# Attention ramp of a hybrid encoder: three shifted copies issued ahead of the rotations, new due times for the rotations and for two value tiles

## The chip, the cores and the metric

The kernel is one program on one core of a Trainium2 chip. The metric is the device time of one execution in microseconds (us). Before the change its median was 1796.95 us of three runs (1796.52 to 1799.05).

## The reference, cut to what matters

A trunk of two layers over 512 tokens and 16 meta tokens (T = 528), width 2048, in float32. Layer 0, which the change touches, is softmax attention with 16 query heads, 8 key and value heads and rotary positions; layer 1 is gated linear attention.

```python
def attention_mixer(h, w_in, q_norm, k_norm, w_out, ang_row, ang_col):
    q, k, v, gate = jnp.split(h @ w_in, [...], axis=-1)
    q = apply_axial_rope(rmsnorm(q, q_norm), ang_row, ang_col)   # per head of 128
    k = apply_axial_rope(rmsnorm(k, k_norm), ang_row, ang_col)
    ...
    s = jnp.einsum('bqkgd,bskd->bkgqs', qb, k) * (ATTN_HEAD_DIM ** -0.5)
    p = jax.nn.softmax(s.astype(jnp.float32), axis=-1).astype(v.dtype)
    o = jnp.einsum('bkgqs,bskd->bqkgd', p, v)
    ...
    return (o * jax.nn.silu(gate)) @ w_out

def rmsnorm(x, w):
    y = xf * lax.rsqrt(jnp.mean(xf * xf, axis=-1, keepdims=True) + NORM_EPS)
    return y * w

def _rotate(x, ang):            # on each half of a head, split in two again
    return jnp.concatenate([x1 * cos - x2 * sin, x2 * cos + x1 * sin], axis=-1)
```

## The kernel before, in words

Every float32 product is made of three fp32r products: each operand is split into a high part (a cast on ACT, L129) and a low part (a subtraction on DVE, L130), and TensorE does high x high, high x low and low x high (L152 to L154). Activations live as `uh`, `ul`, 16 tiles of 128 channels by 528 tokens. `project` (L147 is its weight load) makes one 128-channel tile of an input projection: two halves of 264 columns, for each 16 channel tiles by 3 products, 96 matmuls in all. Its weights come as two units of 512 KB (`wraw`, two buffers), each split into `whi` and `wlo` (three buffers each).

Work beside the projections (softmax, rotations, transposes) is emitted by a clock that the program keeps while it is built: `clk.step` adds the modelled duration of each three matmuls, and `clk.after(dt, fn)` emits `fn` when the modelled time has advanced by `dt`. `tc.high_priority` lets weight splits be placed earlier. After that each engine runs its own list in order; semaphores hold an instruction until its operands, or the buffer it writes, are free.

Layer 0 first makes 13 gate tiles (the last ten by seven products in place of eight, `seven`, L229 to L231), then runs attention in eight groups. A group is one key and value head and two query heads. While group g's softmax runs, the projections of group g+1 (v for g+1 = 1 first, then k, q, q) keep TensorE busy: `qkv` and `values`.

One head's **rotation** is `rope` (L290). With x the projected head and w its norm weight it takes `qw` = w x and `sq` = x squared. Four DMAs on the GpSimd (POOL) queue copy `qw` into `qs` with neighbouring blocks of 32 partitions swapped: the shifted copy (L294). POOL multiplies `qw` by cos (L299) and `qs` by sin (L300). `sq` is split into `sh`, `sl` (one buffer each), and two pairs of matmuls with a matrix of ones, `ssq` (L304, L305), sum it over the head, a pair for each half of the tokens. DVE scales that into `f`, which is `sq` again (L307); ACT makes the inverse root (L133, L134); DVE adds (L311), multiplies (L312), and the result is split into `kh`, `kl` or `qh`, `ql`. `steps` are three due times: first pair of sums, second pair, and the rest (`late`).

The first group has no projections of its own at that point: its k and two q heads (`qws`, three tiles; numbers 94, 95, 96 in the order shown below) were made at the start of the program and wait. `first_group` (L575) squares, scales and rotates them one after the other, 4.2 clock us apart, then yields 9.0 before group 0's softmax. Beside it TensorE runs the v tile and the k tile of group 1. This stretch, from the last `seven` product to the first score matmul (L613), is called the ramp here.

`values(g)` (L540) transposes the projected v tile on TensorE into `vps` and `vpm` (L550, L557), from which ACT and DVE make `vh`, `vl` and `vm` (L553 to L561). Group 0's v tile was projected just before the ramp into the one tile `vt`; group 1's goes into the same `vt`. The transposes and the second pair of `ssq` of the ramp share two PSUM banks (`ps_t`, tag "t"); the first pair of `ssq` uses `ps_o`.

`stored_gates` (L583) loads gate tiles of earlier groups from DRAM into `gr` (two buffers) by DMAs of the SP queue, which also carries all weight loads.

Of the kernel before, what the change touches and what calls it, by code (L numbers as in the profile page):

```python
# [10 lines left out]
F32 = mybir.dt.float32  # L11
F32R = mybir.dt.float32r
I32 = mybir.dt.int32
AF = mybir.ActivationFunctionType
# [5 lines left out]
P = 128  # L20
# [62 lines left out]
def hybrid_encoder(  # L83
# [203 lines left out]
            A.activation(sq[:, a:b], ps, AF.Square)  # L287
        return qw, sq, evac

    def rope(qw, sq, outs, steps, banks):  # L290
        qs = wk.tile([P, T], F32, tag="qs", name="qs")
        for b in range(4):
            s = b ^ 1
            nc.gpsimd.dma_start(out=qs[b * 32:b * 32 + 32, :], in_=qw[s * 32:s * 32 + 32, :])  # L294
        sh = wk.tile([P, T], F32R, tag="sh", name="sh", bufs=1)
        sl = wk.tile([P, T], F32R, tag="sl", name="sl", bufs=1)
        split(sh, sl, sq)
        f = sq
        G.tensor_tensor(qw, qw, cos, op=ALU.mult)  # L299
        G.tensor_tensor(qs, qs, sin, op=ALU.mult)  # L300

        def sums(bank, a, b):
            ps = bank[0].tile([P, 512], F32, tag=bank[1], name="ssq")[:, :b - a]
            PE.matmul(ps, ones_r, sh[:, a:b], start=True, stop=False)  # L304
            PE.matmul(ps, ones_r, sl[:, a:b], start=False, stop=True)  # L305
            with tc.high_priority(AHEAD):
                V.scalar_tensor_tensor(f[:, a:b], ps, 1.0 / P, erow[:, a:b], op0=ALU.mult, op1=ALU.add)  # L307

        def late():
            rsqrt_inplace(f)  # L310
            V.tensor_tensor(qw, qw, qs, op=ALU.add)  # L311
            V.tensor_tensor(qw, qw, f, op=ALU.mult)  # L312
            for hi, lo, a, b in outs:
                split(hi, lo, qw[:, a:b])
        for step, bank, part in zip(steps, banks, HALVES):
            clk.after(step, lambda bank=bank, part=part: sums(bank, *part))
        clk.after(steps[2], late)
# [8 lines left out]
    Q1 = T + META  # L326

    qws = [c0.tile([P, T], F32, name=f"qw{i}") for i in range(3)]
    vt = c0.tile([P, T], F32, name="vt")

    st = ExitStack()
    sp = pool(st, "start")
# [167 lines left out]
    for h in range(3):  # L500
        y = yp.tile([P, T], F32, tag=f"y{h % 2}", name="y")
        project(w_in0, 4096 + h * P, HALVES, lambda ps, a, b: A.copy(y[:, a:b], ps))
        nc.gpsimd.dma_start(out=g_d[h], in_=y)
    project(w_in0, 3072, HALVES, lambda ps, a, b: A.copy(vt[:, a:b], ps))
    clk.finish(built)
    free = [wpool.tile([P, 1024], F32, tag="wraw", name="wraw", bufs=2) for _ in range(2)]
    free += [q[:, :1024] for q in quarters]
# [22 lines left out]
    NP = 3  # L530
    REP = 80
    pn_bufs = [pb.tile([P, T + 96], F32, name=f"pn{i}") for i in range(NP)]
    for t in pn_bufs:
        G.memset(t, 0.0)
    vm_bufs = [pb.tile([REP, P], F32R, name=f"vm{i}") for i in range(2)]
    for t in vm_bufs:
        G.memset(t.bitcast(F32), 0.0)
# [2 lines left out]
    def values(g):  # L540
        vh = wa.tile([P, 4, P], F32R, tag="vh", name="vh")
        vl = wa.tile([P, 4, P], F32R, tag="vl", name="vl")
        vm = vm_bufs[g % 2]
        if g:
            project(w_in0, 3072 + g * P, HALVES, lambda ps, a, b: A.copy(vt[:, a:b], ps))

        def late():
            ps = ps_t.tile([P, 512], F32, tag="t", name="vps")
            for t in range(4):
                PE.transpose(ps[:, t * P:(t + 1) * P], vt[:, t * P:(t + 1) * P], ident)  # L550
            for t in range(4):
                pst = ps[:, t * P:(t + 1) * P]
                A.activation(vh[:, t, :], pst, AF.Copy, scale=rcol[:, t:t + 1])  # L553
                V.scalar_tensor_tensor(vl[:, t, :], pst, rcol[:, t:t + 1], vh[:, t, :].bitcast(F32),
                                       op0=ALU.mult, op1=ALU.subtract)
            pm = ps_t.tile([P, 512], F32, tag="t", name="vpm")[:META, :P]
            PE.transpose(pm, vt[:, SEQ:T], ident)  # L557
            rm = rcol[:META, 4:5]
            A.activation(vm[0:META], pm, AF.Copy, scale=rm)
            A.activation(vm[64:64 + META], pm, AF.Copy, scale=rm)  # L560
            V.scalar_tensor_tensor(vm[32:32 + META], pm, rm, vm[0:META].bitcast(F32),  # L561
                                   op0=ALU.mult, op1=ALU.subtract)
        clk.after(1.2 if g else 2.0, late)
        return vh, vl, vm

    def qkv(g):
        qk, outs = qks[g % 2]
        vv = values(g) if g == 1 else None
        for i, c in enumerate((2048 + g * P, 2 * g * P, (2 * g + 1) * P)):
            qw, sq, evac = take(col(KN if i == 0 else QN))  # L570
            project(w_in0, c, HALVES, evac)
            rope(qw, sq, outs[i], (3.2, 8.8, 9.6), ((ps_p, "pp"), (ps_p, "pp")))
        return qk, vv or values(g)

    def first_group():  # L575
        for i in range(3):
            sq = wk.tile([P, T], F32, tag="sq", name="sq")
            A.activation(sq, qws[i], AF.Square)
            A.activation(qws[i], qws[i], AF.Copy, scale=col(QN if i else KN))
            rope(qws[i], sq, qks[0][1][i], (2.6, 3.9, 8.3), ((ps_o, "o"), (ps_t, "t")))  # L580
            yield 4.2 if i < 2 else 9.0

    def stored_gates(hs, held):  # L583

# [129 lines left out]
    last_gs = [gate(14)]  # L714


    slots = qws + [vt] + [wk.tile([P, T], F32, tag=tag, name="ogr") for tag in ("qs", "sq")]
    NS = len(slots)

    def load_og(k):  # L720
# [694 lines left out]
```

## Time and profile before

| what | value |
|---|---|
| median of three runs | 1796.95 us |
| the profiled execution | 1796.57 us |
| its span in the profile | 1794.8 us |
| TensorE (PE) busy | 1759.3 us |
| VectorE (DVE) busy | 1120.7 us |
| ScalarE (ACT) busy | 946.6 us |
| GpSimd (POOL) busy | 256.6 us |
| mean granted TensorE clock | 0.997 |
| attention groups in the span | from 208.55 to about 800 us |

PE is the matmul stream, PEld its weight loads. A row of the timeline gives the start, the duration, the engine, the line, what is written from what, and in brackets how long the engine had been idle and what ended that. Matmuls overlap: each lasts 0.28 us in the rows, while the next starts about 0.12 us after it, so lost time is read from start to start.

### The profile page before, as it was taken

How to read it: one execution, taken by the hardware profiler on the slowest of the kernel's cores; microseconds unless marked ns; L12 is line 12 of the kernel's file. 1: busy time of each engine (PE TensorE's matmuls, PEld its weight loads, DVE VectorE, ACT ScalarE, POOL GpSimd, SP SyncE). 2: the span in 40 equal slices, each digit the busy share in tenths (PEclk: the TensorE clock that was granted, in tenths of full speed). 3: DMA queues.
4: the chain of work that ended last, by engine and by line, in shares of the span. 5: the costliest groups of instructions: out<-in, count | busy, mean ns of one | idle time of the engine just before them, and what ended most of it. 6: DMA issues, size and time to landing. Idle time of an engine off the chain costs nothing. (4 is left out here: it accounts for less than half of the span.)

```text
span 1794.8 us, 31607 instructions
## 1 busy us (share of the span) xinstructions
PE 1759.3 (98%) x12591; PEld 1655.3 (92%) x12591; DVE 1120.7 (62%) x1904; ACT 946.6 (53%) x1909; POOL 256.6 (14%) x366
## 2 busy tenths in 40 slices
PE   8999989999999999999999999999999999999998
PEld 8999989999999999999999899988898989888886
DVE  5877687667666666732237887667684865764224
ACT  5543466556556454633238544477685765863221
POOL 3000333322312211121111101110000000000000
PEclk9999999999999999999999999999999999999999
DMA  8444423223232233343336444343232333254223
GB/s 254 128 133 124 131 84 102 83 85 107 72 96 84 84 89 91 121 124 89 99 90 207 120 126 133 93 135 96 83 113 83 101 95 89 83 159 176 94 94 129
DMA packets 265252, 200.95 MB, mean 112 GB/s; under 512 B 9772, under 2 KB 239856, under 8 KB 264576
## 3 DMA queue, kind: packets, MB, share of 16 engines
q1 hardware_dynamic: 251888, 159.54, 30.9%
q0 software_dynamic: 13216, 39.39, 6.4%
q8 instruction: 99, 1.62, 0.4%
q14 instruction: 49, 0.40, 0.1%
HBM read 164.39 MB, written 28.01 MB: 107 GB/s over the span
## 5 line engine op out<-in xcount | busy, mean ns | idle before, releaser
L152 PE MATMUL pp<-uh,whi 128*128 128x264 f32 (+1 forms) x2320 | 713.1, 308 | 0.2
L153 PE MATMUL pp<-ul,whi 128*128 128x264 f32 (+1 forms) x2320 | 703.7, 303 | 1.5 <-DVE ul L423 1.5
L154 PE MATMUL pp<-uh,wlo 128*128 128x264 f32 (+1 forms) x2320 | 703.7, 303 | 0.4 <-POOL wlo L362 0.3
L130 DVE TENSOR_TENSOR wlo<-wraw,whi 128x1024 fp32r<-128x1024 f32 (+1 forms) x239 | 292.8, 1226 | 289.6 <-ACT whi L129 286.7
L154 PEld LDWEIGHTS pp<-uh,wlo 128*128 128x128 f32 x2320 | 438.2, 189 | 17.5 <-POOL wlo L362 0.6
L152 PEld LDWEIGHTS pp<-uh,whi 128*128 128x128 f32 x2320 | 438.2, 189 | 16.8 <-ACT uh L422 0.5
L153 PEld LDWEIGHTS pp<-ul,whi 128*128 128x128 f32 x2320 | 438.5, 189 | 15.5 <-DVE ul L423 2.0
L129 ACT CAST whi<-wraw 128x1024 fp32r<-128x1024 f32 (+1 forms) x239 | 248.9, 1042 | 279.2 <-PE pp L153 92.2
L621 ACT ACTIVATE pn<-s,mx 128x528 f32<-128x528 f32 (+1 forms) x72 | 50.2, 697 | 87.5 <-DVE mx L618 87.4
L129 ACT CAST whi<-x 128x1024 fp32r<-128x1024 f32 x48 | 50.1, 1046 | 70.6 <-PE pp L230 52.0
L294 POOL DMA_DIRECT2D qs<-qw x96 | 48.5, 510 | 246.9 <-ACT sq L287 212.3
L1327 PE MATMUL f<-whi,ul 128*128 128x512 f32 x192 | 75.6, 394 | 0.0
L1325 PE MATMUL f<-whi,uh 128*128 128x512 f32 x192 | 75.5, 393 | 0.0
L1326 PE MATMUL f<-wlo,uh 128*128 128x512 f32 x192 | 75.3, 392 | 0.0
L231 PE MATMUL pp<-uh,wlo 128*128 128x264 f32 x264 | 75.2, 285 | 0.0
L229 PE MATMUL pp<-uh,whi 128*128 128x264 f32 x264 | 75.0, 284 | 0.0
L230 PE MATMUL pp<-ul,whi 128*128 128x264 f32 x264 | 74.7, 283 | 0.0
L130 DVE TENSOR_TENSOR wlo<-x,whi 128x1024 fp32r<-128x1024 f32 x48 | 58.6, 1222 | 22.1 <-ACT whi L129 22.1
L311 DVE TENSOR_TENSOR qw<-qw,qs 128x528 f32<-128x528 f32 x24 | 20.0, 835 | 69.1 <-POOL qs L300 69.1
L636 DVE TENSOR_TENSOR pl<-pT,ph 128x512 fp32r<-128x512 f32 (+1 forms) x80 | 47.4, 592 | 16.5 <-ACT ph L635 15.6
L229 PE MATMUL pp<-th,whi 128*128 128x264 f32 x192 | 56.1, 292 | 0.8 <-ACT th L129 0.8
L618 DVE TENSOR_REDUCE mx<-s 128x1 f32<-128x528 f32 (+1 forms) x72 | 50.6, 702 | 9.5 <-PE s L615 8.4
(403 smaller groups left out, 3746.7 us busy)
## 6 DMA issues: line engine op xcount, KB each, us to landing
wraw<-in_attn_w_in_dram SPq DMA_DIRECT2D x82, 512.0 KB, 4.2
wraw<-in_gla_w_in_dram SPq DMA_DIRECT2D x81, 512.0 KB, 3.9
wraw<-in_attn_w_out_dram SPq DMA_DIRECT2D x32, 512.0 KB, 3.8
wraw<-in_gla_w_out_dram SPq DMA_DIRECT2D x32, 512.0 KB, 3.8
x<-in_gla_w_in_dram SPq DMA_DIRECT2D x15, 512.0 KB, 4.3
qs<-qw POOLq DMA_DIRECT2D x96, 66.0 KB, 4.0
x<-in_attn_w_in_dram SPq DMA_DIRECT2D x12, 512.0 KB, 4.6
x<-h_d SPq DMA_DIRECT2D x32, 132.0 KB, 2.9
```

What stands on the lines that cost most here:

```text
L129: A.copy(hi, src)
L130: V.tensor_tensor(lo, src, hi.bitcast(F32), op=ALU.subtract)
L152: PE.matmul(ps, wh, uh[:, k, a:b], start=first, stop=False)
L153: PE.matmul(ps, wh, ul[:, k, a:b], start=False, stop=False)
L154: PE.matmul(ps, wl, uh[:, k, a:b], start=False, stop=last)
L229: PE.matmul(ps, w[0][:, k], bh[:, k], start=k == 0, stop=False)
L230: PE.matmul(ps, w[0][:, k], bl[:, k], start=False, stop=False)
L231: PE.matmul(ps, w[1][:, k], bh[:, k], start=False, stop=k == KH - 1)
L618: V.reduce_max(mx, s, axis=AX.XY, negate=True)
L1325: PE.matmul(ps, uh[:, k, ts], wh[:, kk], start=(k == 0), stop=False)
L1326: PE.matmul(ps, uh[:, k, ts], wl[:, kk], start=False, stop=False)
L1327: PE.matmul(ps, ul[:, k, ts], wh[:, kk], start=False, stop=(k == KT - 1))
```

## The change

Four edits. (1) The four DMAs of a shifted copy move from `rope` into `shifted`, whose tile `qs` gets three buffers in place of two; `first_group` now squares, scales and copies all three heads, then clears the three `pn` tiles, and only then rotates. The third head's squares take one of the two `gr` buffers. (2) The due times of the rotations of the ramp go from (2.6, 3.9, 8.3), 4.2 apart, to (2.6, 4.4, 9.6), 4.6 apart, and softmax starts 9.8 after the last in place of 9.0. (3) Group 0's v tile is transposed at 10.5 clock us in place of 2.0, and group 1's v tile gets the other `gr` buffer (`vt1`) in place of the shared tile. (4) In all later groups the first pair of `ssq` is due 4.0 after its head's projection in place of 3.2. At the end of attention the six tiles that take reloaded data are the same kinds, with "sq" and "qs" in the other order.

```diff
-    def rope(qw, sq, outs, steps, banks):
-        qs = wk.tile([P, T], F32, tag="qs", name="qs")
+    def shifted(qw):
+        qs = wk.tile([P, T], F32, tag="qs", name="qs", bufs=3)
         for b in range(4):
             s = b ^ 1
             nc.gpsimd.dma_start(out=qs[b * 32:b * 32 + 32, :], in_=qw[s * 32:s * 32 + 32, :])
+        return qs
+
+    def rope(qw, sq, outs, steps, banks, qs=None):
+        qs = qs or shifted(qw)
...
-    for t in pn_bufs:
-        G.memset(t, 0.0)
...
+        vt = wa.tile([P, T], F32, tag="gr", name="vt1") if g == 1 else vt0
...
-        clk.after(1.2 if g else 2.0, late)
+        clk.after(1.2 if g else 10.5, late)
...
-            rope(qw, sq, outs[i], (3.2, 8.8, 9.6), ((ps_p, "pp"), (ps_p, "pp")))
+            rope(qw, sq, outs[i], (4.0, 8.8, 9.6), ((ps_p, "pp"), (ps_p, "pp")))
...
     def first_group():
+        sqs, qss = [], []
         for i in range(3):
-            sq = wk.tile([P, T], F32, tag="sq", name="sq")
-            A.activation(sq, qws[i], AF.Square)
+            sqs.append(wk.tile([P, T], F32, tag="sq", name="sq") if i < 2 else
+                       wa.tile([P, T], F32, tag="gr", name="sq"))
+            A.activation(sqs[i], qws[i], AF.Square)
             A.activation(qws[i], qws[i], AF.Copy, scale=col(QN if i else KN))
-            rope(qws[i], sq, qks[0][1][i], (2.6, 3.9, 8.3), ((ps_o, "o"), (ps_t, "t")))
-            yield 4.2 if i < 2 else 9.0
+            qss.append(shifted(qws[i]))
+        for t in pn_bufs:
+            G.memset(t, 0.0)
+        for i in range(3):
+            rope(qws[i], sqs[i], qks[0][1][i], (2.6, 4.4, 9.6), ((ps_o, "o"), (ps_t, "t")), qss[i])
+            yield 4.6 if i < 2 else 9.8
...
-    slots = qws + [vt] + [wk.tile([P, T], F32, tag=tag, name="ogr") for tag in ("qs", "sq")]
+    slots = qws + [vt0] + [wk.tile([P, T], F32, tag=tag, name="ogr") for tag in ("sq",)]
+    slots.append(wk.tile([P, T], F32, tag="qs", name="ogr", bufs=3))
```

What this does to the engines' lists is not what the code's order alone says, so three places are shown. Lines of the changed kernel are 4 higher at L299 and L300 (L303, L304), L304 and L305 (L308, L309), L307, L311 and L312 (L311, L315, L316).

POOL at the ramp, before; `qw_94` is the key head, `qw_95` and `qw_96` the query heads, and `g_d<-y` stores a gate tile:

```order
L294 DMA qs<-qw_94 32x528 x4
L294 DMA qs<-qw_95 32x528
L512 DMA g_d<-y_2148 128x528
L294 DMA qs<-qw_95 32x528
L299 TENSOR_TENSOR qw_94<-qw_94,cos 128x528
L300 TENSOR_TENSOR qs<-qs,sin 128x528
L294 DMA qs<-qw_95 32x528 x2
L299 TENSOR_TENSOR qw_95<-qw_95,cos 128x528
L300 TENSOR_TENSOR qs<-qs,sin 128x528
L601 TENSOR_TENSOR gs<-gs,gr 128x528
L294 DMA qs<-qw_96 32x528 x4
L299 TENSOR_TENSOR qw_96<-qw_96,cos 128x528
```

The same place of POOL after the change:

```order
L294 DMA qs<-qw_94 32x528 x4
L294 DMA qs<-qw_95 32x528
L516 DMA g_d<-y_2148 128x528
L294 DMA qs<-qw_95 32x528 x3
L303 TENSOR_TENSOR qw_94<-qw_94,cos 128x528
L304 TENSOR_TENSOR qs<-qs,sin 128x528
L294 DMA qs<-qw_96 32x528 x4
L303 TENSOR_TENSOR qw_95<-qw_95,cos 128x528
L304 TENSOR_TENSOR qs<-qs,sin 128x528
L303 TENSOR_TENSOR qw_96<-qw_96,cos 128x528
L304 TENSOR_TENSOR qs<-qs,sin 128x528
L610 TENSOR_TENSOR gs<-gs,gr 128x528
```

Two copies of the second head and all four of the third have moved ahead of the second head's multiplications; the third head's copies still stand behind the first head's multiplications. The five clearing instructions ahead of these rows are the same five in both.

DVE at the ramp, before, from the first `vm` on (its rows ahead of that split the k tile's first weights, in both kernels):

```order
L561 SCALAR_TENSOR_TENSOR vm_2412<-vpm,rcol,vm_2412 16x128
L311 TENSOR_TENSOR qw_94<-qw_94,qs 128x528
L307 SCALAR_TENSOR_TENSOR sq<-ssq,erow 128x264
L554 SCALAR_TENSOR_TENSOR vl<-vps,rcol,vh 128x128
L307 SCALAR_TENSOR_TENSOR sq<-ssq,erow 128x264
L554 SCALAR_TENSOR_TENSOR vl<-vps,rcol,vh 128x128
L130 TENSOR_TENSOR sl<-sq,sh 128x528
L591 TENSOR_TENSOR gr<-gr,rrow 128x528
```

The same place of DVE after the change:

```order
L311 SCALAR_TENSOR_TENSOR sq<-ssq,erow 128x264
L315 TENSOR_TENSOR qw_94<-qw_94,qs 128x528
L311 SCALAR_TENSOR_TENSOR sq<-ssq,erow 128x264
L130 TENSOR_TENSOR sl<-sq,sh 128x528
L316 TENSOR_TENSOR qw_94<-qw_94,sq 128x528
L311 SCALAR_TENSOR_TENSOR sq<-ssq,erow 128x264
L130 TENSOR_TENSOR kl_2380<-qw_94,kh_2379 128x528
L315 TENSOR_TENSOR qw_95<-qw_95,qs 128x528
L130 TENSOR_TENSOR wlo<-wraw,whi 128x1024
L311 SCALAR_TENSOR_TENSOR sq<-ssq,erow 128x264
L130 TENSOR_TENSOR sl<-sq,sh 128x528
L315 TENSOR_TENSOR qw_96<-qw_96,qs 128x528
```

The work on the v tiles (L554, L561) and on the gates (L591) has left this stretch; what remains are the rotations and the k tile's second weights.

PE in a later group (the first half's sums of a query head, then the transposes `pT`, `pTm` of softmax rows), before:

```order
L304 MATMUL ssq<-sh,ones_r 128x264
L305 MATMUL ssq<-sl,ones_r 128x264
L152 MATMUL pp<-uh,whi 128x264
L153 MATMUL pp<-ul,whi 128x264
L154 MATMUL pp<-uh,wlo 128x264
L631 MATMUL pT<-ident,pn_2408 128x128 x4
L633 MATMUL pTm<-ident,pn_2408 80x128
```

After the change, from the same matmul on:

```order
L152 MATMUL pp<-uh,whi 128x264
L153 MATMUL pp<-ul,whi 128x264
L154 MATMUL pp<-uh,wlo 128x264
L640 MATMUL pT<-ident,pn_2408 128x128 x4
L642 MATMUL pTm<-ident,pn_2408 80x128
L152 MATMUL pp<-uh,whi 128x264
L153 MATMUL pp<-ul,whi 128x264
L154 MATMUL pp<-uh,wlo 128x264
L308 MATMUL ssq<-sh,ones_r 128x264
L309 MATMUL ssq<-sl,ones_r 128x264
```

The pair of sums now stands six matmuls and five transposes later. From group 2 on the other pairs of sums either stay or stand six matmuls later, and nothing else on PE has moved; beyond attention every engine's list is the same.

More of the change, by code (lines that the diff above doesn't have):

```diff
@@ L328, in hybrid_encoder @@
     qws = [c0.tile([P, T], F32, name=f"qw{i}") for i in range(3)]
-    vt = c0.tile([P, T], F32, name="vt")
+    vt0 = c0.tile([P, T], F32, name="vt0")
     st = ExitStack()
@@ L503, in hybrid_encoder @@
         nc.gpsimd.dma_start(out=g_d[h], in_=y)
-    project(w_in0, 3072, HALVES, lambda ps, a, b: A.copy(vt[:, a:b], ps))
+    project(w_in0, 3072, HALVES, lambda ps, a, b: A.copy(vt0[:, a:b], ps))
     clk.finish(built)
```

## The prediction

> **What bounds the kernel now.** I read the busy times first, then the chain of work that ended last, then TensorE by stretches of time.
>
> ```profile
> PE 1759.3 (98%) x12591; PEld 1655.3 (92%) x12591; DVE 1120.7 (62%) x1904; ACT 946.6 (53%) x1909; POOL 256.6 (14%) x366
> PE 12%; ACT 1%; DVE 0%; DMA 0%; issue 0%; DVEq 0%
> 100.00:200.00 100.00, 100.00 (x825) 100.00 (x824) 72.76 (x83) 36.88 (x41) 4.34 (x8) 1.00 0.38 114
> 208.55:240.60 32.05, 25.37 (x181) 24.52 (x179) 22.37 (x34) 18.27 (x38) 16.67 (x17) 0.89 0.48 139
> 212.84:216.25 3.41, 1.31 (x11) 1.10 (x10) 2.38 (x2) 1.61 (x4) 3.09 (x2) 1.00 0.06 21
> 216.25:219.66 3.41, 3.41 (x18) 3.41 (x18) 2.65 (x6) 1.57 (x4) 1.44 (x3) 0.52 0.83 257
> 226.49:229.90 3.41, 0.36 (x1) 0.19 (x1) 3.41 (x8) 1.10 (x3) 2.01 (x4) 1.00 0.57 162
> 229.90:233.32 3.42, 2.73 (x12) 2.73 (x13) 3.36 (x5) 2.39 (x5) 1.92 (x2) 0.52 0.53 155
> 301.58:305.00 3.42, 1.70 (x14) 1.49 (x13) 3.10 (x5) 2.62 (x6) 0.00 (x0) 1.00 0.00 0
> 305.00:308.41 3.41, 3.41 (x30) 3.41 (x30) 3.28 (x9) 2.61 (x6) 1.14 (x3) 1.00 0.54 157
> ```
>
> PE is busy 98% and makes up the end of the chain too, so only what lets PE wait, or clocks it down, can shorten the kernel. Undisturbed, 825 matmuls fill 100 us: 0.1212 us from start to start. The ramp is the exception. In 32.05 us PE issues 178 instructions by my count of its list (156 projection matmuls, 12 sums, 10 transposes; the row says 181), worth 21.6 us: some 10.5 us are lost. The last six rows show a second loss, the clock: a stretch of 3.41 us with 1.31 or 0.36 us of matmuls is followed by one at 0.52 of full speed (about 1.7 us lost each), one with 1.70 is not.
>
> PE's waits from 243 to 800 us (total, times, longest), and then, from the timeline, the matmuls of the ramp that waited, with the first score matmul:
>
> ```profile
> PE s L613 <- ACT pn L621: 4.3, 6, 1.7
> PE ssq L305 <- DVE sl L130: 2.6, 5, 0.5
> PE pT L631 <- DVE pl L636: 1.4, 2, 1.2
> ...
> 215.97 0.39 PE L304 MATMUL ssq<-sh,ones_r 128*128 128x264 f32 x1 [2.10 <-DVE vm L561]
> 227.36 0.36 PE L304 MATMUL ssq<-sh,ones_r 128*128 128x264 f32 x1 [1.20 <-DVE sq L307]
> 230.59 0.59 PE L305 MATMUL ssq<-sl,ones_r 128*128 128x264 f32 x1 [2.88 <-DVE sl L130]
> 240.60 0.28 PE L613 MATMUL s<-kh,qh 128*128 128x264 f32 x1
> ```
>
> All three waits of the ramp are for DVE, which works one list through: first `vm`, then the first head's sums, then `sl` of the third head behind a weight split.
>
> **Part 1, the ramp (edits 1 to 3).** DVE and POOL take turns:
>
> ```profile
> 205.82 2.01 POOL L294 DMA_DIRECT2D qs<-qw  x4 [0.17 <-issue]
> 213.16 1.30 POOL L299 TENSOR_TENSOR qw<-qw,cos 128x528 f32<-128x528 f32 x1 [2.61 <-DMA qs<-qw]
> 213.50 2.04 DVE L130 TENSOR_TENSOR wlo<-wraw,whi 128x1024 fp32r<-128x1024 f32 x1 [4.31 <-ACT whi L129]
> 214.42 2.29 POOL L300 TENSOR_TENSOR qs<-qs,sin 128x528 f32<-128x528 f32 x1
> 216.66 1.03 POOL L294 DMA_DIRECT2D qs<-qw  x2
> 226.56 2.01 POOL L294 DMA_DIRECT2D qs<-qw  x4 [0.52 <-ACT sh L129]
> 227.75 0.69 DVE L591 TENSOR_TENSOR gr<-gr,rrow 128x528 f32<-128x528 f32 x1
> 228.71 1.21 DVE L130 TENSOR_TENSOR wlo<-wraw,whi 128x1024 fp32r<-128x1024 f32 x1
> 229.85 0.69 DVE L130 TENSOR_TENSOR sl<-sq,sh 128x528 fp32r<-128x528 f32 x1
> 231.22 0.43 DVE L307 SCALAR_TENSOR_TENSOR sq<-ssq,erow 128x264 f32<-128x264 f32 x1
> 233.72 1.83 DVE L312 TENSOR_TENSOR qw<-qw,sq 128x528 f32<-128x528 f32 x1
> ```
>
> The same `wlo` takes 1.21 us alone and 2.04 beside POOL: it starts to work when cos ends (214.46) and ends at 215.54, and POOL's sin, 2.29 instead of 1.30, starts only then. DVE at L312 stretches from 0.7 to 1.83 likewise, while L307, which reads PSUM, keeps 0.43. So of two instructions with both operands in SBUF, one waits for the whole other. The Trainium skill ("SBUF — State Buffer", section "Who interferes with whom") says just this of DVE's tensor_tensor and GpSimd, a lock for the whole instruction; it speaks against this change, which puts three heads' multiplications back to back; by it this part gains 3.1, without it 8.0 (both worked out below from rows).
>
> The changed order, walked. The first cos waits for copies issued earlier, so it stays at 213.16; two more copies (1.03) lie in POOL's 2.61 of waiting. `wlo` ends at 215.54 and sin at 216.71; then L311 and L307, and `sl` of the second head ends at 218.45. The v tile's transposes and its `vm` are gone from here, so PE does not stop at 213.9. It reaches the sum that needs `sl` after 71 instructions, at 208.55 + 71 × 0.1212 = 217.15: **first wait 1.3**. POOL then issues the third head's four copies (2.01, to 218.75), and from there cos and sin of heads two and three (four of 1.30) alternate with DVE's L312 (0.70), `kl` (0.65), L311 (0.60), the k tile's second `wlo` (1.20) and L307 (0.40): 5.2 + 3.55 from 218.75 is 227.5. PE needs that last L307's bank for `vpm`, where it stands at 222.6: **second wait 4.9**. The stretch 223.08 to 226.49 is then empty, and PE runs at half speed from 227.5 to 229.90: **1.2**. Together 7.4.
>
> The first score matmul now stands 15 projection matmuls later, after 193 instructions (23.4 us). Before, that work would take 32.05 + 15 × 0.1212 = 33.9; now 23.4 + 7.4 = 30.8. **Gain 3.1.** With each multiplication at its short length the same walk has waits of 0.4, 1.15 and 0.95 and no slow stretch: gain 8.0. At the other end the multiplications displace one more sum, for one or two more slow stretches (1.7 each): gain 1.4 to below nothing (-0.3). I take 3.1, since the stretched rows stand in this very place.
>
> Given back: the gates' multiplications (L591) leave the ramp for group 0's softmax, whose `gr` loads wait until the other uses of `gr` are done. POOL's five clearings stay ahead of the first copy: nothing. The weight loads queued behind `gr` on SP are needed some 20 us later: nothing. For DVE's later start in group 0 I charge **0.6**, one L591 (0.69), with bounds 0 and 1.7 (the longest wait of a score matmul for exp, above). Part 1 in sum: **2.5**.
>
> **Part 2, 4.0 in place of 3.2.** The later groups lose at one place each, five times:
>
> ```profile
> 414.89 0.28 PE L154 MATMUL pp<-uh,wlo 128*128 128x264 f32 x1
> 415.11 0.39 PE L304 MATMUL ssq<-sh,ones_r 128*128 128x264 f32 x1
> 416.01 0.39 PE L305 MATMUL ssq<-sl,ones_r 128*128 128x264 f32 x1 [0.51 <-DVE sl L130]
> 416.23 0.28 PE L152 MATMUL pp<-uh,whi 128*128 128x264 f32 x1
> 427.07 0.29 PE L613 MATMUL s<-kh,qh 128*128 128x264 f32 x1
> ...
> 414.92 0.29 DVE L638 TENSOR_TENSOR pmt<-pTm,pmt 16x128 fp32r<-16x128 f32 x1
> 415.24 0.71 DVE L130 TENSOR_TENSOR sl<-sq,sh 128x528 fp32r<-128x528 f32 x1
> ```
>
> From 414.89 to 416.23 are 1.34 us where three starts should take 0.36: 0.98 lost, though the wait says 0.51. The pair now stands six matmuls and five transposes later (some 1.3 us), so PE reaches it at about 416.3 to 416.5, and `sl` is done at 415.95. What is late next: `pT`, now 1.2 us earlier, whose DVE operands are done at 415.21; then nothing before the next score matmul, at 427.07. 5 × 0.98 = 4.9; I take **4.7**, for a `pT` that waits a little; bounds 1 (it waits as `ssq` did) and 5.
>
> **Part 3, the boundary of groups 0 and 1.**
>
> ```profile
> 281.01 0.29 PE L305 MATMUL ssq<-sl,ones_r 128*128 128x264 f32 x1
> 302.80 0.28 PE L154 MATMUL pp<-uh,wlo 128*128 128x264 f32 x1
> 304.80 0.39 PE L613 MATMUL s<-kh,qh 128*128 128x264 f32 x1 [1.72 <-ACT pn L621]
> ...
> 286.38 0.71 DVE L130 TENSOR_TENSOR ql<-qw,qh 128x528 fp32r<-128x528 f32 x1
> ```
>
> The second score of group 1 waits for an exponential and loses 2.00 - 0.12 = 1.88. In the changed order 98 PE instructions instead of some 41 lie between first and second score, so that goes. But the first score now stands 46 instructions (5.1 to 5.6 us) after the pair of sums whose head it reads, and from that pair to the end of `ql` it takes 287.09 - 281.01 = 6.1: a new wait of about 1.0. **Gain 0.9**, bounds -1.9 and 1.9.
>
> **Sum.** 2.5 + 4.7 + 0.9 = 8.1 off the profiled 1796.57 us (its span 1794.8, with 1.8 around it): 1788.5. That execution lies 0.4 below the median, which I leave in the range. What this kernel's measurement can tell from no change is about 0.2%, 3.6 us: faster begins below 1793.4.
>
> **Rivals.** (a) *The waits of the ramp only move.* Two more slow stretches (3.4) eat the 3.1: about 1791 to 1792. For it: 1.31 us of matmuls in a stretch were not enough to keep the clock, and the second wait is twice as long as the longest now. Against: the walk has the slow stretch in it already, and three blocked places become two. The Trainium skill ("TensorE: Matmul & The Clock Gate", section "What's actually happening") has half rate follow a whole idle window; here one with 1.31 us of matmuls was enough, so the measurement decides; by that rule (a) would need two more empty stretches, and my sum, whose stretch is empty, stays.
>
> (b) *POOL and DVE don't meet.* If the splits fall into POOL's pauses, the ramp gains up to 8.0: 1783.6. Against: every pair of rows that overlaps in the ramp is stretched.
>
> (c) *The step to 4.0 doesn't pay*, because `pT` or the next pair waits in place of `ssq`: gain 1 or less, about 1792 to 1793. For it: `pT L631` waited before, 1.2 us at most. With (a) together: some 1796, no change.
>
> (d) *Slower: the copies land late.* The first four copies were issued from 205.82 to 207.83 and the first cos started at 213.16, 5.3 us on, while weights and cos and sin tables were under way. Now up to twelve copies share that time. Each us that cos starts later passes to sin, L311, `sl` and PE's first and second wait. From 8.1 us late the gain is used up, and at 12 us it is 1796.57 - 8.1 + 12 = 1800.5. Against: the first head's copies are still ahead of all others on their queue.
>
> (e) *It doesn't do what it says*: the third head's copies stand behind the first head's multiplications on POOL, not first. That is in the walk: without it those 2.01 us before the second cos would go.
>
> **How the numbers follow.** Forecast 1788.5 with 0.52; (a) 0.17, (b) 0.07, (c) 0.12, of which half below 1793.4, (a) with (c) 0.06, (d) 0.06. Faster: 0.52 + 0.17 + 0.07 + 0.06 = 0.82; no change 0.06 + 0.06 = 0.12; slower 0.06. The range leaves out (d), (a) with (c) and the better half of (b), and takes in (c) and most of the bounds: 1784.5 to 1794.0.
>
> **What would show it.** Right: the first two sums of the ramp without a wait for `vm`; a wait of 1 to 1.5 us near 217 for `sl` and one of 4 to 5 near 223 for L307's result, with one stretch at half clock behind it; no wait of L309 for `sl` after 300 us; the wait for exp at 304.8 gone, and about 1 us at the first score of group 1. Wrong: a slow stretch more or none (part 1 by 1.7 or more), five waits of `pT` near 0.5 us (part 2), or a first cos later than 213.5 (rival d).

## The result and the profile after

| | before | changed |
|---|---|---|
| median of 15 runs each | 1798.20 us | 1801.32 us |
| lowest to highest | 1795.35 to 1799.58 | 1798.70 to 1807.04 |
| profiled execution | 1796.57 us | 1803.56 us |

The ratio is 1.0021, 95% interval 1.0013 to 1.0029: slower by some 3.8 us, where 8.1 us of gain were forecast. The profiled execution of the changed kernel is 2.2 us above its median, that of the kernel before 1.6 us below, so the two traces differ by 7.0 us where the medians differ by 3.1. Two executions of all those on record, one of the kernel before (1892 us) and one of the version called "changed, all three" below (4421 us), were far off the others and are left out of the ratios and of that version's median.

The page of the changed kernel begins as before; PE is as busy, in a longer span:

```profile
span 1801.8 us, 31618 instructions
...
PE 1759.4 (98%) x12591; PEld 1655.7 (92%) x12591; DVE 1125.4 (62%) x1904; ACT 946.1 (53%) x1909; POOL 256.3 (14%) x366
```

PE's timeline in the changed kernel, at the places that the prediction speaks of (start, duration, and in brackets the wait):

```profile
219.42 0.59 PE L309 MATMUL ssq<-sl,ones_r 128*128 128x264 f32 x1 [2.51 <-DVE sl L130]
227.56 0.28 PE L560 MATMUL vpm<-ident,vt 128*16 128x128 f32 x1 [2.47 <-DVE sq L311]
239.12 0.29 PE L622 MATMUL s<-kh,qh 128*128 128x264 f32 x1
...
304.66 0.59 PE L622 MATMUL s<-kh,qh 128*128 128x264 f32 x1 [2.32 <-ACT pn L630]
...
418.21 0.29 PE L309 MATMUL ssq<-sl,ones_r 128*128 128x264 f32 x1
...
431.35 0.44 PE L553 MATMUL vps<-ident,vt 128*128 128x128 f32 x2 [1.26 <-ACT vt L548]
```

The ramp came out as forecast in its total. The waits stand where they were put (for `sl`, and for the bank of L311 before `vpm`), with other sizes, and the first score matmul, with 15 projection matmuls more ahead of it, starts at 239.12 in place of 240.60. From the last `seven` matmul (at 208.43 before, 208.02 now) that is 31.10 us for work that took 32.17 + 1.82: 2.9 us gained, 3.1 forecast.

The rest was lost behind it. At 304.66 a score matmul of group 1 waits longer than before and starts when it did before (304.80). At 418.21 the wait of `ssq` is gone, as forecast, but 13 us later the v tile's transposes, `vps`, wait 1.26 us for the copy of `vt`, which at this place they didn't do before. PE's waits in the changed kernel from 310 to 800 us:

```profile
PE s L622 <- ACT pn L630: 6.0, 5, 1.8
PE vps L553 <- ACT vt L548: 5.1, 5, 1.3
```

Before, the same stretch had 2.6 us of `ssq` waits, 2.4 of score waits and 0.5 on `vps`. Five waits of one kind were exchanged for five of another, and the score waits grew. The stretches of 3.41 us, with PE's share and the granted clock (third column from the right), show one more loss:

```profile
216.25:219.67 3.42, 0.91 (x7) 0.70 (x6) 2.61 (x4) 1.45 (x3) 3.40 (x6) 0.90 0.73 215
219.67:223.08 3.41, 3.41 (x19) 3.41 (x20) 3.06 (x3) 1.58 (x2) 3.41 (x3) 0.60 0.06 18
301.59:305.00 3.41, 1.09 (x8) 0.88 (x7) 2.59 (x5) 1.49 (x5) 0.00 (x0) 0.90 0.04 14
305.00:308.41 3.41, 3.41 (x19) 3.41 (x19) 3.29 (x6) 2.48 (x6) 1.26 (x3) 0.60 0.60 170
```

The wait at 304.66 leaves 1.09 us of matmuls in its stretch, and PE runs at half speed behind it, up to 1.7 us more (before, that stretch had 1.70 us of matmuls and kept its clock).

### The profile page after: what moved, and what is told of

It reads as the page before. It is cut to its first block, busy times and chain, and to the rows that moved or that the text cites. A ratio compares the mean times of both kernels' runs of the same rounds, so it can differ in the third digit from the quotient of the medians.

```text
span 1801.8 us, 31618 instructions
## 1 busy us (share of the span) xinstructions
PE 1759.4 (98%) x12591; PEld 1655.7 (92%) x12591; DVE 1125.4 (62%) x1904; ACT 946.1 (53%) x1909; POOL 256.3 (14%) x366
## 5 line engine op out<-in xcount | busy, mean ns | idle before, releaser
L315 DVE TENSOR_TENSOR qw<-qw,qs 128x528 f32<-128x528 f32 x24 | 18.7, 780 | 76.0 <-POOL qs L304 76.0
```

## The experiments

"To the 7th" and "7th to last" below are read off PE's timeline: the time from the last `seven` matmul to the 7th of the 32 matmuls that multiply `vm` (late in group 1), and from there to the 32nd, the end of attention. The same work lies between these points in all kernels. Behind each, in brackets, is how many stretches of 3.41 us at half clock fell in it. One execution each, up to 6 us from its kernel's median ("before, 4.0, three gs": 1795.51 against 1801.42), so small differences between rows of the last two columns mean little; the ratios are against the kernel before as run beside each. The names in the first column are explained where each run is told; "both" is vt on DVE and gate first, "all three" these with the sum on POOL.

| kernel | ratio to before, interval | to the 7th | 7th to last |
|---|---|---|---|
| before | 1 | 136.0 (2) | 408.5 (0) |
| changed | 1.0021, 1.0013 to 1.0029 | 137.5 (2) | 413.9 (1) |
| edits 1 to 3 | 1.0011, 1.0000 to 1.0022 | 137.9 (2) | 411.2 (1) |
| edit 4 alone | 1.0016, 1.0008 to 1.0025 | 136.4 (3) | 412.3 (1) |
| edits 1 and 2 | 1.0017, 1.0006 to 1.0027 | 137.2 (2) | 411.5 (1) |
| changed, v tiles later | 1.0031, 1.0019 to 1.0042 | 134.6 (2) | 414.3 (0) |
| before, 4.0, three gs | 1.0023, 1.0014 to 1.0033 | 136.5 (2) | 407.1 (0) |
| before, three gs | 1.0004, 0.9995 to 1.0013 | 138.0 (3) | 407.3 (0) |
| changed, three gs | 1.0035, 1.0023 to 1.0048 | 137.7 (2) | 411.3 (0) |
| edits 1 to 3, three gs | 1.0011, 1.0002 to 1.0021 | 138.2 (3) | 407.5 (0) |
| before, 4.0, vt on DVE | 1.0008, 0.9999 to 1.0016 | 136.4 (2) | 410.6 (1) |
| changed, vt on DVE | 1.0015, 1.0006 to 1.0024 | 135.3 (1) | 414.6 (1) |
| changed, gate first | 1.0015, 1.0006 to 1.0024 | 134.3 (1) | 412.8 (1) |
| changed, both | 1.0007, 0.9998 to 1.0016 | 135.0 (2) | 411.9 (1) |
| before, 4.0, sum on POOL | 0.9982, 0.9973 to 0.9990 | 139.1 (3) | 404.0 (0) |
| before, sum on POOL | 0.9968, 0.9956 to 0.9981 | 138.0 (3) | 401.5 (0) |
| changed, sum on POOL | 0.9966, 0.9956 to 0.9976 | 136.7 (2) | 404.9 (1) |
| changed, all three | 0.9931, 0.9918 to 0.9944 | 133.5 (1) | 398.3 (0) |
| the same, step 3.2 | 0.9947, 0.9935 to 0.9960 | 134.7 (1) | 401.9 (1) |
| the same, old ramp | 0.9955, 0.9942 to 0.9969 | 139.7 (4) | 398.6 (0) |

### Which part loses

The changed kernel with the step 3.2 (edits 1 to 3):

```diff
-            rope(qw, sq, outs[i], (4.0, 8.8, 9.6), ((ps_p, "pp"), (ps_p, "pp")))
+            rope(qw, sq, outs[i], (3.2, 8.8, 9.6), ((ps_p, "pp"), (ps_p, "pp")))
```

> The changed kernel with the first pair of sums due 3.2 after its projection again (edits 1 to 3 alone). Theory A: in groups 3 to 7 the step 4.0 only lays bare a chain on ACT, POOL and DVE (end of a projection, gate, multiplications, copy of the v tile) that was as long as PE's own way with its 0.98 us wait in it, and makes that chain 0.5 us longer; so the changed kernel's five waits of vps for the copy of vt (1.1 to 1.5 us) go, the five waits of ssq for sl (0.98 us from start to start) come back, and the time falls by 2 to 5 us against the changed kernel, to within 2 us of the kernel before. Rival B: the loss arises in group 0 alone (gates and their loads moved into its softmax), and the step 4.0 gains as predicted; then this kernel is 3 to 5 us slower than the changed one, some 1805.

Measured 1.0011, some 2.0 us above before. The `ssq` waits are back (five, 2.6 us), the `vps` waits are 1.0 us (two), as theory A has it. Rival B's 1805 us is excluded; the ramp's own part doesn't gain either, though (0 to 4 us of loss).

The kernel before with the step 4.0 alone (the same line, the other way):

> The kernel before with the step 4.0 alone. Theory A: the five waits of ssq for sl go and five waits of vps for the copy of vt of 0.9 to 1.5 us appear; slower than before by 1 to 5 us. The prediction's part 2 (rival B): 4.7 us faster than before.

Measured 1.0016, some 2.9 us slower, where the prediction's part 2 gave 4.7 us of gain. Its waits of PE from 310 to 800 us begin:

```profile
PE vps L550 <- ACT vt L545: 6.1, 6, 1.4
PE s L613 <- ACT pn L621: 3.2, 5, 0.8
```

So neither part gains: 2.0 us are lost by the one (an interval that reaches down to nothing) and 2.9 by the other, together about the change's 3.8 within the intervals. Edits 1 and 2 without 3 (step 3.2 and):

```diff
-        vt = wa.tile([P, T], F32, tag="gr", name="vt1") if g == 1 else vt0
+        vt = vt0
...
-        clk.after(1.2 if g else 10.5, late)
+        clk.after(1.2 if g else 2.0, late)
```

> Edits 1 and 2 alone: the changed kernel with the step 3.2, group 0's v tile due at 2.0 and group 1's v tile in the shared tile again. Theory A says that the ramp's gain of 2.9 us is given back in group 0 because gate loads wait for the two gr buffers until the second v tile is transposed: here gate loads wait only for the third head's squares, the score matmul near 304.7 waits less than 2.3 us, and the boundary's stretch at half clock is not there; the v transposes are back in the ramp, whose waits are as long as before or longer. Time within 2 us of the kernel with edits 1 to 3. Rival D: the losses of group 0 come from the three rotations and their spacing, and stay (waits above 2 us near 304.7).

Measured 1.0017. The score at the boundary of groups 0 and 1 still waits 2.23 us: rival D. The boundary's wait is not due to the `gr` buffer that the v tile borrows (the third head's squares still borrow the other). The half-clock stretch behind it is not there in this trace, as theory A had it.

### Where the wait goes when it is moved

The changed kernel with the v tiles of groups 2 to 7 transposed later:

```diff
-        clk.after(1.2 if g else 10.5, late)
+        clk.after(10.5 if g == 0 else 1.2 if g == 1 else 2.6, late)
```

> The changed kernel with the v tiles of groups 2 to 7 transposed 2.6 clock us after their projection in place of 1.2 (12 matmuls later on PE). Theory A: the copy of vt is then done when PE comes to vps; the five waits (5.1 us) go, and the time falls by 3 to 6 us against the changed kernel. Rival C: DVE and ACT as a whole are late there, and the next score matmul waits for them instead: no gain, within 1 us of the changed kernel.

Measured 1.0031: rival C, if anything worse (the intervals overlap). No wait of `vps` is left, but waits of score matmuls for exp (7.8 us, 6.0 before this edit) and 3.9 us of `pTm` for `vl` stand in its place.

Three `gs` buffers (in the kernels with edits 1 to 3 the third head's shifted copy takes the third, since there is no room for more):

```diff
-        gs = wa.tile([P, T], F32, tag="gs", name="gs", bufs=2)
+        gs = wa.tile([P, T], F32, tag="gs", name="gs", bufs=3)
```

> The kernel before with the step 4.0 and three gs buffers in place of two. Theory A2: the copy of vt, for which vps waits 1.2 to 1.5 us in groups 3 to 7 of the step 4.0 alone, is late because on ACT's list the gate's first instruction (L137) ahead of it waits some 1.5 us for a gs buffer, which the multiplication of o_sb (L595) frees; that stands on DVE behind L311, which waits for POOL's rotation, and this one was made later by the step. With a third buffer that wait goes: vps waits 0.3 us or less, the ssq waits are gone too, and the time is 3 to 6 us below the kernel before. Rival C2: ACT and DVE are late as a whole (the copies' landing and L311 set the time): vps still waits 1 us or more, and the time stays 2 to 4 us above the kernel before.

> The kernel before with three gs buffers alone (step 3.2). Theory A2: the five ssq waits (0.98 us from start to start) stay, and ACT's waits for a gs buffer in groups 3 to 7 were covered: no gain there; at the boundary of groups 0 and 1 the gate may start earlier and the third score of group 1 wait less than 1.7 us. In sum 0 to 2 us faster. Rival: the third buffer by itself is what gains, 3 us or more.

> The changed kernel with three gs buffers (the third head's shifted copy takes one of them, and qs has two). Theory A2: at the boundary of groups 0 and 1 the gate's L137 no longer waits 3.6 us for the multiplication of o_sb, so the next gate tile is loaded earlier, the reduction behind it on DVE is not held, and the third score of group 1 waits under 1 us instead of 2.3, without a stretch at half clock; in groups 3 to 7 vps waits 0.3 us or less. Time 5 to 9 us below the kernel before. Rival C2: both waits stay, time as the changed kernel, 3 to 4 us above the kernel before.

> Edits 1 to 3 with the step 3.2 and three gs buffers. Theory A2: the boundary of groups 0 and 1 is mended as with the step 4.0, the five ssq waits (4.9 us) stay: 1 to 4 us below the kernel before, and 3 to 5 us above the same with 4.0. Rival C2: 1 to 3 us above the kernel before, as edits 1 to 3 with two buffers.

Theory A2's forecasts fail. With 4.0 the time stays above before (1.0023), though `vps` waits less in the one trace (3.6 us in all); alone the third buffer gains nothing (1.0004); in the changed kernel the boundary's wait shrinks to 1.12 us, and a wait of `pT`, 2.56 us for a normalization on DVE (L633), appears at 257 us (1.0035); with 3.2 it is 1.0011, as without the buffer. With the third buffer the whole series of gates runs one place earlier, and ACT's gate still waits for the same multiplication on DVE (kernel before with 4.0 and three buffers):

```profile
424.93 0.65 ACT L137 ACTIVATE gs<-gr 128x528 f32<-128x528 f32 x1 [1.48 <-DVE o_sb L595]
```

So the intended wait was not removed, and these runs say only that a buffer more does not help; whether that wait makes `vt` late they leave open. Next, the copy of `vt` off ACT's list, and the gate's multiplication earlier on DVE's:

```diff
-            project(w_in0, 3072 + g * P, HALVES, lambda ps, a, b: A.copy(vt[:, a:b], ps))
+            project(w_in0, 3072 + g * P, HALVES, lambda ps, a, b: V.tensor_copy(vt[:, a:b], ps))
```

> The kernel before with the step 4.0, and the copy of each v tile (vt) made by DVE in place of ACT; TensorE's list is that of the step 4.0 alone, row for row. Theory A3: what makes vps wait is vt's place on ACT's list, behind the gate (L137 to L139) and the inverse root, whose operands come late through POOL's rotation, L311 and L595; DVE has a pause of 2 us there, so the five waits of vps fall from 1.2 to 1.5 us to 0.5 or less and the time comes out 1 to 4 us below the kernel before. Rival C: ACT and DVE as a whole are late at this place; the time lost on vps comes back as waits of score matmuls for exp and of pTm for vl (as with the v tile transposed later), and the time stays 2 to 4 us above the kernel before.

> The changed kernel with the copy of each v tile made by DVE. Theory A3: groups 3 to 7 lose 4 to 6 us less than in the changed kernel, the boundary of groups 0 and 1 stays as it is (third score of group 1 waits 2 us or more): 3 to 6 us below the changed kernel, near the kernel before. Rival C: no change against the changed kernel.

```diff
-            V.tensor_tensor(og, og, gs, op=ALU.mult)
+            with tc.high_priority():
+                V.tensor_tensor(og, og, gs, op=ALU.mult)
```

> The changed kernel with high priority for the gate's last multiplication (L604), so that on DVE the first of each group's two stands some rows earlier (ahead of the split of the squares in place of behind it). Theory B2: at the boundary of groups 0 and 1 the ramp's gain is lost because the chain copies, rotation, L315, gate, gate load, reduction, exp sets when the third score can start; with the first gate's multiplication earlier, POOL's gate product is out of the way of L315, the next gate tile is loaded 1 to 2 us earlier and the third score of group 1 waits 0.7 us or less in place of 2.3; vps waits in groups 3 to 7 shrink by up to 0.5 us each. 3 to 6 us below the changed kernel. Rival: the wait of the third score stays above 1.5 us, and the time within 1.5 us of the changed kernel.

> The changed kernel with both: v tiles copied by DVE, and the gate's last multiplication with high priority. If theories A3 and B2 hold, their gains add: 6 to 10 us below the changed kernel, 3 to 6 us below the kernel before. Rival C: within 2 us of the changed kernel.

With `vt` on DVE the `vps` waits are gone, and most of the waiting comes back at the score matmuls (kernel before with 4.0 and `vt` on DVE, 310 to 800 us):

```profile
PE s L613 <- ACT pn L621: 7.4, 9, 1.1
```

In place of 6.1 + 3.2 us of waits there are 7.4: the ratio falls from 1.0016 to 1.0008, with intervals that overlap. In the changed kernel the same edit gives 1.0015. With the gate first, also 1.0015, the boundary's score waits 1.60 us in place of 2.32 (the rival's side of the mark). Both together bring the changed kernel to 1.0007. Each of these takes back a little at most, and the change still doesn't pay.

### What holds PE

What the score waits have in common is seen on DVE. The changed kernel in group 2: the end of a score on PE, DVE's next instructions, the exponential on ACT, and the next score:

```profile
401.90 0.28 PE L624 MATMUL s<-kl,qh 128*128 128x264 f32 x1
...
405.51 0.71 DVE L315 TENSOR_TENSOR qw<-qw,qs 128x528 f32<-128x528 f32 x1 [4.04 <-POOL qs L304]
406.14 0.70 DVE L627 TENSOR_REDUCE mx<-s 128x1 f32<-128x528 f32 x1
...
406.87 0.70 ACT L630 ACTIVATE pn<-s,mx 128x528 f32<-128x528 f32 x1 [3.53 <-DVE mx L627]
...
407.72 0.39 PE L622 MATMUL s<-kh,qh 128*128 128x264 f32 x1 [0.99 <-ACT pn L630]
```

The score is complete at 402.2, and its reduction could start. It stands behind L315, the sum of the rotation, which waits 4.04 us for POOL's sin product, and that for the copies; so exp and the next score are late. DVE has no work in these 4.04 us: it is L315's wait, not its 0.71 us of work, that holds the reduction. The gate's multiplication stands behind the next L315 likewise, and ACT's list with `vt` behind that:

```profile
424.98 0.71 DVE L315 TENSOR_TENSOR qw<-qw,qs 128x528 f32<-128x528 f32 x1 [3.33 <-POOL qs L304]
...
427.02 0.65 ACT L137 ACTIVATE gs<-gr 128x528 f32<-128x528 f32 x1 [1.51 <-DVE o_sb L604]
...
430.94 0.36 ACT L548 COPY vt<-pp 128x264 f32<-128x264 f32 x1
```

DVE's largest wait from 310 to 800 us, before and in the changed kernel (total, times, longest):

```profile
DVE qw L311 <- POOL qs L300: 61.0, 18, 5.0
```

```profile
DVE qw L315 <- POOL qs L304: 74.3, 18, 6.3
```

The test takes only this instruction off DVE, from group 1 on. Against the step 4.0 alone, PE's and ACT's lists stay the same row for row:

```diff
-            V.tensor_tensor(qw, qw, qs, op=ALU.add)
+            (G if banks[0][1] == "pp" else V).tensor_tensor(qw, qw, qs, op=ALU.add)
```

> The kernel before with the step 4.0, and from group 1 on the sum of the rotation (L311: qw plus the shifted copy times sin) made by POOL in place of DVE; the lists of TensorE and ACT are those of the step 4.0 alone, row for row, and DVE's lacks L311. Theory D: PE's lost time in groups 2 to 7 is set by DVE's list, where L311 waits 2.5 to 4 us for POOL (for the copies' landing, cos and sin) and holds the reductions and the gate multiplications behind it, and through these ACT's gate, inverse root and vt; the step 4.0 took a wait of PE that lay beside this. Then the waits of score matmuls for exp (3.2 us in all from 310 to 800) fall below 1.5, the waits of vps for vt from 6.1 us to 2 or less, and the time comes out 3 to 8 us below the kernel before. Rival E: the chain itself (copies, cos, sin, sum, L312) is what is late, not what stands behind L311 on DVE: with 0.6 us more per sum on POOL the waits stay or grow, time 2 to 6 us above the kernel before.

> The kernel before with the sum of the rotation on POOL from group 1 on, step 3.2. Theory D: the waits of score matmuls for exp fall, the five ssq waits (4.9 us) stay: 1 to 4 us below the kernel before, and 3 to 5 us above the same with 4.0, so that the step is worth what the prediction gave it once DVE's list is free. Rival E: 0 to 3 us above the kernel before, and the step 4.0 on top of it a loss again.

> The changed kernel with the sum of the rotation on POOL from group 1 on. Theory D: also the third score of group 1 waits less than 1 us (2.3 in the changed kernel), since the gate's second multiplication and the reduction no longer stand behind L315, and the ramp's 2.9 us are kept: 6 to 11 us below the changed kernel, 1 to 4 below the kernel before with step 4.0 and the sum on POOL. Rival E: the third score still waits 2 us or more, time within 2 us of the changed kernel.

> The changed kernel with v tiles copied by DVE, the gate's last multiplication with high priority, and the sum of the rotation on POOL from group 1 on. Theory D: the fastest of all, 5 us or more below the kernel before. Rival E: no better than without the sum on POOL, within 2 us of the kernel before.

Theory D holds for the score and `ssq` waits. The sum takes longer on POOL (1.33 us in place of 0.71) and the kernel before gets faster by 0.32%, with 4.0 from 1.0016 to 0.9982, changed from 1.0021 to 0.9966. No score matmul waits for exp any more from 310 to 800 us. Three marks were missed. With 4.0, `vps` still waits 4.0 us (2 were expected). In the kernel before with the sum on POOL the five `ssq` waits don't stay: none is left, so they too were DVE's lateness, and 3.2 seems the better step there (7th to last 401.5 against 404.0; the ratios' intervals overlap). And the boundary's score of the changed kernel waits 1.98 us (1 was expected; with the old ramp it waits 3.2 to 3.4 us in these versions, 1.72 in the kernel before).

So with this one sum moved, all four edits together are worth nothing: 0.9966 with them, 0.9968 without. L311 explains what held PE before the change, but not by itself why the change didn't pay. Where `vps` still waits, the trace of the kernel before with 4.0 and the sum on POOL shows DVE's list held by another operand, a gate load:

```profile
424.74 1.03 DVE L591 TENSOR_TENSOR gr<-gr,rrow 128x528 f32<-128x528 f32 x1 [4.25 <-DMA gr<-g_d]
425.69 0.70 DVE L595 TENSOR_TENSOR o_sb<-o_sb,gs 128x528 f32<-128x528 f32 x1
```

DVE waits 14.7 us for such loads from 310 to 800 us (five times; 0.8 us with the sum on DVE). ACT's gate waits for L595 in turn, and the copy of `vt` stands behind the gate. No run was made that loads the gate tiles earlier.

With `vt` on DVE and the gate first as well, next to nothing is left (310 to 800 us):

```profile
PE s L623 <- ACT pn L631: 1.0, 1, 1.0
PE pTm L643 <- DVE vl L557: 0.3, 1, 0.3
PE pT L641 <- DVE pl L646: 0.2, 1, 0.2
PE pp L152 <- DVE gr L617: 0.2, 1, 0.2
```

and the reduction waits for nothing but its score:

```profile
397.21 0.71 DVE L628 TENSOR_REDUCE mx<-s 128x1 f32<-128x528 f32 x1 [1.17 <-PE s L625]
```

Its median is 1784.84 us against 1798.52: 0.69% faster (0.56 to 0.82), the fastest of all. Two more runs ask what the change's own parts are worth there:

> The fastest version (sum of the rotation on POOL, v tiles copied by DVE, gate's last multiplication first, all four edits) with the step 3.2 in place of 4.0. Theory D: the ssq waits of the kernel before were DVE's list held by L311 as well, and with the list free they don't come back, as with the sum on POOL alone: within 1.5 us of the fastest version, so edit 4 is worth nothing. Rival F: they come back (4.9 us): 3 to 5 us slower than the fastest version.

> The kernel before with the step 4.0, the sum of the rotation on POOL from group 1 on, v tiles copied by DVE and the gate's last multiplication first: the fastest version without edits 1 to 3. Theory D: with DVE's list free the ramp's gain is kept, so this is 3 to 6 us slower than the fastest version, and all of that lies ahead of 340 us. Rival G: the ramp's gain is swallowed at the boundary of groups 0 and 1 here too: within 1.5 us of the fastest version.

Going back to 3.2 costs 0.16% (0.9947 against 0.9931), some 2.9 us; two of five `ssq` waits come back, 0.9 us together, so neither side of that expectation is met in full, and the intervals overlap by a little. Going back to the old ramp costs 0.24%, some 4.3 us, with intervals that just touch, and all of it lies ahead of the 7th mark (139.7 against 133.5); behind it the two agree to 0.3 us. In that one execution the old ramp has four slow stretches and the new one one, which is 5.1 of the 6.2 us. Part of that lies at the boundary: its score waits 3.30 us with the old ramp and 1.45 with the new one.

## Why the prediction was wrong

**The step that failed.** "Only what lets PE wait, or clocks it down" was right, but the prediction then took each wait for something local, to be removed where it stands: "what is late next" was asked of the next operand (`pT`: "then nothing before the next score matmul"), not of the lists on which all operands come. That gave 4.7 us of gain for part 2 and 0.9 for part 3. Measured alone, part 2 loses 2.9 us, with 6.1 us of `vps` waits; part 3's wait grew from 1.72 to 2.32 us, with a stretch at half clock behind it. Most of PE's waits in groups 2 to 7 went back to DVE's list held behind L311 (61 us of waiting in total, visible in the same trace as DVE's own largest wait, which the prediction doesn't list): with the sum on POOL, PE's waits from 310 to 800 us fall from 7.5 to 3.5 us in the kernel before, and from 13.0 to 5.5 in the changed kernel. What is left in the changed kernel is mostly `vps` (3.5 us), which waits for ACT's list.

**Part 1, the ramp: right in its total.** The gain at the first score was 2.9 against 3.1. The walk put the end of the second wait at 227.5, and it ended at 227.56. How the loss ahead of that is divided came out otherwise: the first wait was 2.51 us in place of 1.3, since `sl` took 1.47 us and ended at 219.37 (218.45 in the walk), the slow stretch followed this wait and not the second, and the second, which PE reached later, was 2.47 in place of 4.9. That 227.5 was met is in part luck: the walk let POOL and DVE alternate, and they didn't (last section). A wait of 0.51 us for `vm` is in both ramps (at 236.24 before, 232.09 after) and was not counted.

**Given back.** The 0.6 charged for group 0 became the whole gain. From the last `seven` matmul to the third score of group 1 the same 686 PE instructions take 96.64 us, 96.37 before. By the 7th mark the changed kernel was 1.5 us behind, not 3.4 ahead (3.1 - 0.6 + 0.9).

**Part 3, the boundary: wrong.** The score at 304.80 is the third of group 1, not the second; the 98 PE instructions that were to cover it lie ahead of the second, and between second and third there are 41, as before. (The new wait at the first score, forecast at 1.0, cost about 0.6.) In the changed kernel the third score waits for a reduction behind a gate tile's load:

```profile
292.85 2.44 DVE L315 TENSOR_TENSOR qw<-qw,qs 128x528 f32<-128x528 f32 x1
295.21 0.70 DVE L604 TENSOR_TENSOR o_sb<-o_sb,gs 128x528 f32<-128x528 f32 x1
...
302.46 0.71 DVE L600 TENSOR_TENSOR gr<-gr,rrow 128x528 f32<-128x528 f32 x1 [0.81 <-DMA gr<-g_d]
303.09 0.70 DVE L627 TENSOR_REDUCE mx<-s 128x1 f32<-128x528 f32 x1
```

L315 (2.44 us beside POOL), the gate's multiplication, ACT's gate, POOL's product that frees `gr`, the load, and L600 stand ahead of the reduction, which ends at 303.79. In the kernel before it ended at 302.96, but its exponential came only behind a weight cast on ACT's list:

```profile
302.26 0.70 DVE L618 TENSOR_REDUCE mx<-s 128x1 f32<-128x528 f32 x1
...
302.91 1.04 ACT L129 CAST whi<-wraw 128x1024 fp32r<-128x1024 f32 x1
303.96 0.69 ACT L621 ACTIVATE pn<-s,mx 128x528 f32<-128x528 f32 x1
```

So two different chains release the third score at nearly the same time, and that just the ramp's gain was lost there is, as far as these traces show, a coincidence. The stretch at half clock (up to 1.7 us) comes on top; the bound of -1.9 left it out.

**Part 2, the step 4.0: wrong in place.** The `ssq` waits went, as forecast, and `pT` took no harm. What had been lost there came back at `vps` and the scores: in its effect rival (c), to which 0.12 was given, though (c) named `pT` or the next pair, and its price was too small, since the time also got longer. With the sum on POOL, `vt` off ACT's list and the gate first, the step gains some 2.9 us, of 4.7 forecast, with intervals that overlap by a little; with the sum on POOL alone it seems to cost 2.5 (0.9982 against 0.9968, intervals that overlap too). Which of the other two edits it needs was not tried.

**The rivals and the range.** The forecast needs both parts to be kept. In the version with all three they are, 4.3 and 2.9 us. That this comes near the 8.1 forecast is partly luck, since the 4.3 includes what the boundary costs the old ramp in that version, and with the sum on POOL alone the four edits are worth nothing. Of the rivals, only (c) came, in its effect; (a), (b) and (d) did not: the first cos started at 213.30, and the ramp kept its gain up to the first score. None of the rivals had the waits tied together by one list, so the range ended at 1794.

**Open.** Why the changed kernel spreads from 1798.7 to 1807.0 us was not tried by a run of its own. The traces of all kernels have one to four slow stretches ahead of the 7th mark and up to one behind, up to 1.7 us each. A stretch of 3.41 us at half clock lowers the mean granted clock of an execution by 0.001. Over the 15 executions of the changed kernel that mean goes from 0.998 and 0.997 (the five fastest) to 0.995 (the slowest), which would be two or three stretches, some 3 to 5 of the 8.3 us; the rest stays open.

## What to carry to other kernels

Before moving a wait of the bounding engine, list the largest waits of the engines that feed it: an in-order list that is held by one slow operand makes everything behind it late together, and a local wait removed from the bounding engine can come back at the next operand of that list. A sum that waits for another engine's product may do better on that other engine, even where it takes nearly twice as long, as here. Once one such hold is gone, look for the next: here the gate loads and the copy of `vt` held what the sum no longer did. And one experiment that left PE's and ACT's lists untouched and moved a single instruction told more here than several that moved the wait.

## What the runs showed of the hardware

The walk let POOL and DVE alternate, one instruction each. In the changed kernel they did not: a split of DVE of a kind that takes 0.69 to 0.71 us alone sat out the rest of one POOL product and two more. The views are POOL's and DVE's timelines.

```profile
220.49 1.78 POOL L304 TENSOR_TENSOR qs<-qs,sin 128x528 f32<-128x528 f32 x1
222.23 1.32 POOL L303 TENSOR_TENSOR qw<-qw,cos 128x528 f32<-128x528 f32 x1
223.52 1.31 POOL L304 TENSOR_TENSOR qs<-qs,sin 128x528 f32<-128x528 f32 x1
```

```profile
221.78 3.62 DVE L130 TENSOR_TENSOR kl<-qw,kh 128x528 fp32r<-128x528 f32 x1 [0.35 <-ACT kh L129]
```

It ended at 225.40, 0.57 us after POOL's last product (224.83). The Trainium skill ("SBUF — State Buffer", section "SBUF: two separate sides") lets whichever starts first hold the shared ports for its whole instruction, while the other is blocked; that agrees for one instruction. Here two further POOL products, one right behind the other, went ahead of a split that had already begun, which took 2.9 us longer than alone. In the kernel before, a waiting weight split did get in between cos and sin (213.50 to 215.54).

The clock shows in all twenty traces together. In the stretches of 3.41 us as the changes of the granted clock delimit them, between 200 and 1700 us, each of the 40 with less than 1.6 us of PE busy time was followed by one at half clock; of those with 1.6 us or more, ten were (1.67 to 2.46 us), and others with 1.60 or 1.64 us were not. So short stops that leave a stretch over half empty cost up to 1.7 us more here, and where PE's busy time is longer, it alone doesn't tell.
